# Other places in SBUF for the tiles that TensorE reads, in a one-core layer of attention, recurrence and MLP

## The chip, the cores and the metric

The kernel runs on one core of a Trainium2 chip. The metric is the device time of one execution in microseconds (us); the median of three runs is given, and lower is better.

## What is computed

One decoder layer for 256 tokens of width 1024, in fp32. All of its large products are of the form activations times weights, and the weights are 74 MB:

```python
proj = jnp.einsum("bsd,dc->bsc", u, w_in)          # 1024 x 7168
q, k, v, x_lru, g_lru, gate_attn, gate_lru = jnp.split(proj, list(SPLITS), axis=-1)
attn = moba_attention(qh, kh, to_heads(v))         # 8 heads x 128
y_attn = attn @ w_branch_attn
xc = causal_depthwise_conv(x_lru, conv_w, conv_b)
hl = rg_lru(xc, w_rg_a, b_rg_a, w_rg_i, b_rg_i, lru_lambda)
y_lru = (hl * jax.nn.gelu(g_lru)) @ w_branch_lru
merged = jax.nn.sigmoid(gate_attn) * y_attn + jax.nn.sigmoid(gate_lru) * y_lru
h = h + rms_norm(merged @ w_out, attn_post_norm[l])
u = rms_norm(h, mlp_pre_norm[l])
m = jnp.square(jax.nn.relu(u @ w_mlp_up[l])) @ w_mlp_down[l]
h = h + rms_norm(m, mlp_post_norm[l])
```

## The kernel before

**Chunks.** The weights come in 74 chunks of 1 MB, 2048 fp32 numbers on each of 128 partitions. `load` (L65) fetches a chunk into one of three `wraw` tiles. `split` (L75) cuts it exactly into an upper part `whi` (ScalarE, L89; VectorE, L87, for six chunks) and the rest `wlo` (VectorE, L90). There are three `whi` and three `wlo` tiles, used in turn, so that chunk c and chunk c + 3 have the same ones. `ahead` (L95) issues loads up to three chunks and the split one chunk before the products.

**Products.** Activations are kept as an upper and a lower part too, for instance `xgh` and `xgl` (the normed input), `xch` and `xcl` (after the convolution), `ath` and `atl` (attention), `lrh` and `lrl` (recurrence), `mgh` and `mgl` (merged), `u2` (input of the MLP, both parts side by side), `rrh` and `rrl` (the MLP's inside). A product is three matmuls of type float32r: upper with upper, and the two mixed ones. A matmul has a stationary operand of 128 columns, loaded ahead of it (PEld in the profile), and a moving operand of 256 or 512 columns, which stream through. All of them lie in SBUF as rows of fp32 along each partition.

- `three` (L152 to L155), used by `feat_chunk` (L167), the first chunk and the gates `r` and `i`: the weights are stationary and 256 tokens move: 48 matmuls with 256 columns in each chunk.
- `v_chunk` (L193) and `tok_products` (L465 to L467): activations are stationary and weights move. A chunk of `v` or of the output projection has 24 matmuls with 512 columns; one of the down projection has 18 with 512 columns and 12 with 256.
- `up_tokens` (L572 to L574): the same for the first 512 columns of the up projection. In the loop of L596 weights are stationary again; per block there is one matmul with 512 columns (L606: both parts of `u2` with `whi`) and one with 256 (L607: the upper part with `wlo`), so 16 and 16 in a chunk.

So in every chunk 12,288 columns stream through TensorE: 2048 matmuls with 256 columns and 752 with 512 in all. The scores, the transposes and the products of attention with `v` are plain fp32 and not among them.

**Places.** Five SBUF pools lie one behind the other in the order of their creation (L43 to L49): `const`, `slot` (one place for each tag `s0`, `s1`, ...; several tiles share a place at different times), `wraw`, `whi`, `wlo`; then `tmp` and `small`. Within a pool, places follow each other in the order in which they are first asked for. The sizes of the tiles alone set their addresses. A step from one block of the contraction to the next is 1024 bytes in all operands, and the second half of a chunk's output features lies 512 bytes further; so an operand's offset modulo 512 is that of its tile.

Of the kernel before, what the change touches and what calls it, by code (L numbers as in the profile page):

```python
# [9 lines left out]
F32 = mybir.dt.float32  # L10
F32R = mybir.dt.float32r
# [4 lines left out]
P = 128  # L16
T = 256
D = 1024
# [4 lines left out]
MASK_VALUE = -1e30  # L23

# chunks of weights, 1 MB each, in their order of use
# (x_lru and v in turns)
C_XL, C_V, C_Q, C_K, C_RGA, C_RGI = 0, 1, 8, 12, 16, 17
C_GL, C_GA, C_GEL, C_BA, C_BL, C_OUT, C_UPT, C_UP, C_DN = 18, 22, 26, 30, 34, 38, 42, 44, 58
NCHUNK = 74

# the part of a chunk whose upper half is taken by the vector engine instead of the scalar engine
HI_ON_VECTOR = {c: 1.0 for c in range(17, 23)}

# columns of the channel-major parameters (8 columns each)
(P_W0, P_W1, P_W2, P_W3, P_CB, P_BA, P_BI, P_LAM, P_G1, P_G2) = range(0, 80, 8)
NPAR = 80


@with_exitstack
def hybrid_layer(ctx: ExitStack, tc: tile.TileContext, head_d, x_d, w_d, cst_d, gp_d, out_d):  # L40
    nc = tc.nc

    const = ctx.enter_context(tc.tile_pool(name="const", bufs=1))  # L43
    slot = ctx.enter_context(tc.tile_pool(name="slot", bufs=1))
    wraw_p = ctx.enter_context(tc.tile_pool(name="wraw", bufs=3))
    whi_p = ctx.enter_context(tc.tile_pool(name="whi", bufs=3))
# [4 lines left out]
    ps_at = ctx.enter_context(tc.tile_pool(name="ps_at", bufs=4, space=PSUM))  # L51

    def slot_tile(i, name, dt=F32, shape=(P, KB, T)):
        return slot.tile(list(shape), dt, tag=f"s{i}", name=name)

# [5 lines left out]

# [1 line left out]
    raws, splits = {}, {}  # L63
# [7 lines left out]

    # chunks whose parts stay longer lie in tiles that are free by then
    own_slots = {C_OUT + 2: (8, 10), C_OUT + 3: (5, 6)}

    def split(c):  # L75
        raw, parts = raws.pop(c)
        if c in own_slots:
            hi, lo = (slot_tile(i, f"w{c}_{i}", F32R, (P, 2048)) for i in own_slots[c])
        else:
            hi = whi_p.tile([P, 2048], F32R, tag="whi", name=f"whi{c}")  # L80
            lo = wlo_p.tile([P, 2048], F32R, tag="wlo", name=f"wlo{c}")
        n = 2048 // parts
        for i in range(parts):
            s = slice(i * n, (i + 1) * n)
            k = i * n + int(n * HI_ON_VECTOR.get(c, 0))
            if k > i * n:
                nc.vector.tensor_copy(hi[:, i * n:k], raw[:, i * n:k])  # L87
            if k < (i + 1) * n:
                nc.scalar.copy(hi[:, k:(i + 1) * n], raw[:, k:(i + 1) * n])  # L89
            nc.vector.tensor_tensor(lo[:, s], raw[:, s], hi[:, s].bitcast(F32), ALU.subtract)  # L90
        splits[c] = (hi, lo)
# [3 lines left out]
    def ahead(c):  # L95
        """loads and splits that run ahead of the products with chunk c"""
        while state["load"] < min(NCHUNK, c + 4):
            load(state["load"])
            state["load"] += 1
        while state["split"] < min(NCHUNK, c + 2):  # L100
            with tc.high_priority():
                split(state["split"])
            state["split"] += 1

# [1 line left out]
    eps = const.tile([P, 1], F32, name="eps")  # L106
    nc.vector.memset(eps, EPS)
    first = small.tile([P, 1], F32, tag="warm", name="first")
    nc.scalar.copy(first, eps)
    # parameters, then by block of the contraction: x, features on partitions, and chunk 0 of the weights  # L110
    head = const.tile([P, NPAR + 512], F32, name="head")
# [14 lines left out]
    make_identity(nc, ident)  # L126
    # mask[q, 128 + k] = k <= q ? 0 : MASK_VALUE
    mask = const.tile([P, 2 * P], F32, name="mask")
# [8 lines left out]
    xgl = slot_tile(2, "xgl", F32R)  # L137
    whi0 = whi_p.tile([P, 2048], F32R, tag="whi", name="whi0")
    wlo0 = wlo_p.tile([P, 2048], F32R, tag="wlo", name="wlo0")
    for kb in range(KB):  # L140
        x, w = xw[kb][:, 0:T], xw[kb][:, T:512]
# [8 lines left out]

# [1 line left out]
    def three(out, wh, wl, xh, xl, start, stop):  # L152
# [4 lines left out]
    def first_chunk(xh, xl):  # L157
        """the same, block by block of the contraction, as the operands arrive"""
        hi, lo = splits.pop(0)
        banks = [mm_bank(f"mm0_{o}")[:, 0:T] for o in range(2)]  # L160
        for kb in range(KB):
            for o in range(2):
                s = slice(kb * 256 + o * P, kb * 256 + (o + 1) * P)
                three(banks[o], hi[:, s], lo[:, s], xh[:, kb, :], xl[:, kb, :], kb == 0, kb == KB - 1)
        return banks

    def feat_chunk(c, xh, xl, urgent=False):  # L167
        """two blocks of output features, [P features, 2, T]; unless what follows is urgent, the next split precedes it"""
        ahead(c + 1)
        hi, lo = splits.pop(c)  # L170
        hi = hi.rearrange("p (k c) -> p k c", k=KB)
        lo = lo.rearrange("p (k c) -> p k c", k=KB)
        bank = mm_bank(f"mm{c}").rearrange("p (o t) -> p o t", o=2)
        for o in range(2):
            for kb in range(KB):
                s = slice(o * P, (o + 1) * P)
                three(bank[:, o, :], hi[:, kb, s], lo[:, kb, s], xh[:, kb, :], xl[:, kb, :],
                      kb == 0, kb == KB - 1)
        if not urgent:
            ahead(c + 2)  # L180
        return bank

    # x_lru and the causal convolution
    PADW = T + 4
# [4 lines left out]
    xcl = slot_tile(6, "xcl", F32R)  # L189
    # v, tokens on partitions  # L190
    vt = slot.tile([P, 2, D], F32, tag="s11", name="vt")
# [61 lines left out]

    # sp8 = 8 softplus(-lam) = 8 (max(-lam, 0) + log1p(exp(-|lam|))), log1p(z) = 2 atanh(z / (2 + z))
    lam = par[:, P_LAM:P_LAM + 8]
# [23 lines left out]

    # q, k with rotary positions on features 0..31 of each head  # L280
    # (rows 0..31 of all heads are brought together as [4 x 32, 2 heads, T] for it)
    swap = list(range(16, 32)) + list(range(16))
# [19 lines left out]

    # r, i gates
    rt = slot_tile(7, "rt")
# [16 lines left out]

    # RG-LRU: a = exp(-sp8 r), mult^2 = -expm1(-2 sp8 r) = tanh(sp8 r) (1 + a^2)
    mult = slot_tile(3, "mult")
# [25 lines left out]

    # attention, one head in steps  # L350
    ath = slot_tile(12, "ath", F32R)
# [43 lines left out]

    # the three gates, with the attention of one head between chunks
    gL = slot_tile(4, "gL")
# [28 lines left out]

    # branch projections; merged = 0.5 (1 + tanh(gL / 2)) y_lru + 0.5 (1 + tanh(gA / 2)) y_attn
    mgh = slot_tile(1, "mgh", F32R)
# [18 lines left out]

# [1 line left out]
    halves = (slice(0, 512), slice(512, 1024))  # L449

    def tok_products(c0, n, act, parts):
        """act(kb) -> (hi, lo) of [P, T]; the last two chunks go one part of the result at a time"""
        acc = [[at_bank(f"acc{c0}_{b}{i}") if i < 2 else mm_bank(f"acc{c0}_{b}{i}") for i in range(len(parts[b]))]
# [31 lines left out]
    class TokenNorm:  # L485
        """1 / sqrt(mean(y^2) + eps) per token, y in parts"""

# [18 lines left out]

    # output projection, post norm, residual; then the next norm's input, features on partitions
    # (both parts of a block side by side, [P, T upper | T lower])
    u2 = [slot_tile(i, f"u2_{i}", F32R, (P, 4, 512)) for i in (12, 3)]
# [36 lines left out]
    def square_of_norm(b):  # L546
        """the norm's factor enters relu(.)^2 as its square, per token, after the down projection"""
        n = TokenNorm("h", 2)
        for i in range(2):
            r2 = n.part(i, x_tok[:, b, halves[i]])  # L550
        nc.vector.tensor_tensor(scl2[:, b:b + 1], r2, r2, ALU.mult)
# [5 lines left out]

# [1 line left out]
    rrh = [slot_tile(i, f"rrh{i}", F32R) for i in (4, 1, 2, 5)]  # L559
    rrl = [slot_tile(i, f"rrl{i}", F32R) for i in (7, 6, 8, 10)]  # L560

    # the first 512 columns with tokens on partitions, one block of tokens at a time
    ahead(C_UPT + 1)
# [69 lines left out]
def _rotary(np):  # L633
    """cosines and signed sines for rows 0..31 of a head, four times over"""
    inv = np.float32(500000.0) ** (-np.arange(0, 32, 2, dtype=np.float32) / np.float32(32))
    ang = (np.arange(T, dtype=np.float32)[:, None] * inv[None, :].astype(np.float32)).T
    cos = np.concatenate([np.cos(ang)] * 2)
    sin = np.concatenate([-np.sin(ang), np.sin(ang)])
    return np.tile(np.stack([cos, sin], axis=1), (4, 1, 1)).astype(np.float32)


def _pack(np, inp):
    """layout only: pieces of the inputs in the order and the form in which the chip reads them"""
    def a(name):
# [70 lines left out]
```

## Time and profile before

| | us |
|---|---|
| median of 3 runs | 449.8 (448.93, 449.80, 449.89) |
| span of the profiled execution | 447.7 |
| profiled execution's own time beside the median | 2.1 less: the span runs from its first to its last instruction |

The profile is of one execution. Its page gives busy time by engine, the granted clock of TensorE in 40 slices, and the chain of work that ended last. Views of the trace that are used here: the waits of one engine, and busy times in stretches of the span. The "busy" of a matmul in these views runs from its start to the modelled end of its drain, and successive matmuls overlap; how fast TensorE works is therefore read from the distance between starts, or from the length of a stretch that holds a known number of matmuls.

### The profile page before, as it was taken

The numbers are of one execution on the slowest core, as the hardware profiler recorded it, in microseconds if no ns is written. First come the engines' busy times: TensorE is split into PE (matmuls) and PEld (weight loads), VectorE is DVE, ScalarE is ACT, GpSimd is POOL, SyncE is SP. The second block draws the span as 40 slices with busy tenths as digits, with TensorE's granted clock in tenths as the row PEclk, the third lists the DMA queues.
The fourth block names the chain that finished last, engine by engine and source line by source line (L and its number), as shares of the span: only waits on it lengthen the run. The fifth ranks groups of instructions, "written<-read, shape, count | busy, mean of one in ns | idle before, by whom it ended". The sixth has DMA issues, their size and how long they took to land.

```text
span 447.7 us, 7026 instructions
## 1 busy us (share of the span) xinstructions
PE 437.3 (98%) x2916; PEld 402.2 (90%) x2916; DVE 302.2 (67%) x383; ACT 241.0 (54%) x342; POOL 21.5 (5%) x48
## 2 busy tenths in 40 slices
PE   6999999999999999999999999999999999999994
PEld 6999999999999999999998878888888888888884
DVE  5749975779997666885688566777777744444425
ACT  6686743409897575553556475555555433333322
POOL 1000073202000000000000000000000000000000
PEclk9999999999999999999999999999999999999999
DMA  8977555655634356355567703455555545455202
GB/s 269 408 286 284 180 204 206 215 202 194 208 122 167 122 194 233 120 182 189 187 219 258 277 0 132 171 190 184 192 182 188 188 182 192 184 188 193 83 1 94
DMA packets 14575, 83.59 MB, mean 187 GB/s; under 512 B 1808, under 2 KB 2576, under 8 KB 5456
## 3 DMA queue, kind: packets, MB, share of 16 engines
q1 hardware_dynamic: 13520, 80.39, 49.9%
q0 software_dynamic: 736, 2.36, 1.5%
q8 instruction: 23, 0.38, 0.3%
q10 hardware_dynamic: 288, 0.39, 0.2%
q14 instruction: 8, 0.07, 0.0%
HBM read 81.04 MB, written 1.05 MB: 183 GB/s over the span
## 4 chain that ended last, share of the span: by engine, by line
PE 97%; DMA 1%; ACT 0%; DVE 0%; issue 0%; DVEq 0%; ACTq 0%
PE mm L153 14%; PE mm L154 14%; PE mm L155 14%; PE up L606 12%; PE acc L467 8%; PE acc L466 8%; PE acc L465 8%; PE up L607 6%; PE v L204 2%; PE v L203 2%; PE v L202 2%; PE up L574 1%; PE up L572 1%; PE rg L153 1%; PE rg L155 1%; PE rg L154 1%
## 5 line engine op out<-in xcount | busy, mean ns | idle before, releaser
L90 DVE TENSOR_TENSOR wlo<-wraw,whi 128x2048 fp32r<-128x2048 f32 (+2 forms) x78 | 163.6, 2100 | 89.5 <-ACT whi L89 89.3
L89 ACT CAST whi<-wraw 128x2048 fp32r<-128x2048 f32 (+2 forms) x72 | 125.3, 1740 | 127.8 <-PE acc L467 44.4
L153 PE MATMUL mm<-xgh,whi 128*128 128x256 f32 x384 | 109.8, 290 | 4.2 <-ACT xgh L144 4.2
L154 PE MATMUL mm<-xgl,whi 128*128 128x256 f32 x384 | 109.1, 284 | 0.0
L155 PE MATMUL mm<-xgh,wlo 128*128 128x256 f32 x384 | 108.9, 284 | 0.0
L606 PE MATMUL up<-u,whi 128*128 128x512 f32 x224 | 78.9, 396 | 0.0
L153 PEld LDWEIGHTS mm<-xgh,whi 128*128 128x128 f32 x384 | 72.7, 191 | 4.6 <-ACT xgh L144 4.2
L154 PEld LDWEIGHTS mm<-xgl,whi 128*128 128x128 f32 x384 | 73.4, 191 | 0.5
L155 PEld LDWEIGHTS mm<-xgh,wlo 128*128 128x128 f32 x384 | 73.4, 191 | 0.0
L607 PE MATMUL up<-u,wlo 128*128 128x256 f32 x224 | 63.0, 281 | 0.0
L467 PE MATMUL acc<-whi,rrl 128*128 128x512 f32 (+1 forms) x160 | 56.0, 350 | 0.0
L466 PE MATMUL acc<-wlo,rrh 128*128 128x512 f32 (+1 forms) x160 | 55.8, 349 | 0.0
L465 PE MATMUL acc<-whi,rrh 128*128 128x512 f32 (+1 forms) x160 | 55.7, 348 | 0.0
L606 PEld LDWEIGHTS up<-u,whi 128*128 128x128 f32 x224 | 42.1, 188 | 9.9
L607 PEld LDWEIGHTS up<-u,wlo 128*128 128x128 f32 x224 | 42.3, 189 | 0.0
L466 PEld LDWEIGHTS acc<-wlo,rrh 128*128 128x128 f32 x160 | 30.1, 188 | 4.4
L465 PEld LDWEIGHTS acc<-whi,rrh 128*128 128x128 f32 x160 | 30.2, 189 | 4.3
L467 PEld LDWEIGHTS acc<-whi,rrl 128*128 128x128 f32 x160 | 30.1, 188 | 4.1
L153 PE MATMUL mm<-lrh,whi 128*128 128x256 f32 x64 | 18.1, 283 | 0.0
L154 PE MATMUL mm<-lrl,whi 128*128 128x256 f32 x64 | 18.1, 283 | 0.0
L155 PE MATMUL mm<-lrh,wlo 128*128 128x256 f32 x64 | 18.1, 283 | 0.0
L154 PE MATMUL mm<-atl,whi 128*128 128x256 f32 x64 | 18.0, 282 | 0.0
(197 smaller groups left out, 640.8 us busy)
## 6 DMA issues: line engine op xcount, KB each, us to landing
wraw<-in_w_dram SPq DMA_DIRECT2D x70, 1024.0 KB, 4.8
wraw<-in_w_dram SPq DMA_DIRECT2D x8, 256.0 KB, 6.5
xw_a<-in_head_dram SPq DMA_DIRECT2D x4, 256.0 KB, 3.9
wraw<-in_w_dram SPq DMA_DIRECT2D x2, 512.0 KB, 7.0
x_tok<-in_x_dram SPq DMA_DIRECT2D x1, 1024.0 KB, 9.2
gp<-in_gp_dram POOLq DMA_DIRECT2D x1, 1024.0 KB, 4.6
xw_b<-in_head_dram SPq DMA_DIRECT2D x3, 256.0 KB, 4.6
out_dram<-res ACTq DMA_DIRECT2D x2, 192.0 KB, 2.0
```

The costliest lines, as they stand in the source:

```text
L89: nc.scalar.copy(hi[:, k:(i + 1) * n], raw[:, k:(i + 1) * n])
L90: nc.vector.tensor_tensor(lo[:, s], raw[:, s], hi[:, s].bitcast(F32), ALU.subtract)
L153: nc.tensor.matmul(out, wh, xh, start=start, stop=False)
L154: nc.tensor.matmul(out, wh, xl, start=False, stop=False)
L155: nc.tensor.matmul(out, wl, xh, start=False, stop=stop)
L202: nc.tensor.matmul(banks[b], xgh[:, kb, s], hi[:, k, :], start=kb == 0, stop=False)
L203: nc.tensor.matmul(banks[b], xgh[:, kb, s], lo[:, k, :], start=False, stop=False)
L465: nc.tensor.matmul(out, xh[:, s], hi[:, hs], start=first, stop=False)
L466: nc.tensor.matmul(out, xh[:, s], lo[:, hs], start=False, stop=False)
L467: nc.tensor.matmul(out, xl[:, s], hi[:, hs], start=False, stop=last)
L606: nc.tensor.matmul(bank, hi[:, kb, c], u2[kb // 4][:, kb % 4, :], start=kb == 0, stop=False)
L607: nc.tensor.matmul(bank[:, 0:T], lo[:, kb, c], u2h(kb, slice(0, T)), start=False, stop=kb == KB - 1)
```

## The change

The change allots unused gaps in front of some tiles, and makes the `whi` and `wlo` tiles 64 bytes (16 numbers) longer than what is used of them, so that the three places of each step by 64 bytes modulo 1024. No instruction, shape, wait or order on any engine is different; only SBUF addresses are. Gaps are counted in units of 32 bytes.

```diff
+GAPS = {"const": 1, "s10": 4, "s8": 8, "s12": 1, "whi": 15, "wlo": 26}
+W_STEP = 16
...
+    def gap(pool, tag):
+        if tag in GAPS:
+            pool.tile([P, 8 * GAPS[tag]], F32, tag="gap_" + tag, name="gap_" + tag, bufs=1)
+    laid = set()
     def slot_tile(i, name, dt=F32, shape=(P, KB, T)):
+        if i not in laid:
+            laid.add(i)
+            gap(slot, f"s{i}")
         return slot.tile(list(shape), dt, tag=f"s{i}", name=name)
...
+    gap(const, "const")
+    gap(whi_p, "whi")
+    gap(wlo_p, "wlo")
...
+    def weight_tiles(c):
+        hi = whi_p.tile([P, 2048 + W_STEP], F32R, tag="whi", name=f"whi{c}")
+        lo = wlo_p.tile([P, 2048 + W_STEP], F32R, tag="wlo", name=f"wlo{c}")
+        return hi[:, 0:2048], lo[:, 0:2048]
...
-            hi = whi_p.tile([P, 2048], F32R, tag="whi", name=f"whi{c}")
-            lo = wlo_p.tile([P, 2048], F32R, tag="wlo", name=f"wlo{c}")
+            hi, lo = weight_tiles(c)
...
-    whi0 = whi_p.tile([P, 2048], F32R, tag="whi", name="whi0")
-    wlo0 = wlo_p.tile([P, 2048], F32R, tag="wlo", name="wlo0")
+    whi0, wlo0 = weight_tiles(0)
```

Where the tiles begin, in bytes of a partition modulo 1024, worked out from the sizes of all tiles in front of them:

| tiles | before | after |
|---|---|---|
| `whi`, `wlo`, chunks 0, 3, 6, ... | 224 | 128 |
| `whi`, `wlo`, chunks 2, 5, 8, ... | 224 | 192 |
| `whi`, `wlo`, chunks 1, 4, 7, ... | 224 | 256 |
| `xgh`, `xgl`, `mgh`, `mgl`, `atl`, second half of `u2`, three of the four `rrh` | 96 | 128 |
| `xch`, `xcl`, `lrh`, `lrl`, the last `rrh`, one `rrl` | 224 | 256 |
| two `rrl` | 224 | 384 |
| one `rrl` | 224 | 640 |
| `ath`, first half of `u2` | 224 | 672 |

The three sequences of chunks hold up to chunk 39; two later chunks of the output projection lie in places of `slot`, and from chunk 42 on the numbers are shifted. Before, all of these offsets leave 32 modulo 64; after, all but 672 are multiples of 64.

## Rows read from the trace of the kernel before

**Rows 1.** The page: span, busy time of each engine (share, instructions), TensorE's granted clock, chain.

```profile
span 447.7 us, 7026 instructions
...
PE 437.3 (98%) x2916; PEld 402.2 (90%) x2916; DVE 302.2 (67%) x383; ACT 241.0 (54%) x342; POOL 21.5 (5%) x48
...
PEclk9999999999999999999999999999999999999999
...
PE 97%; DMA 1%; ACT 0%; DVE 0%; issue 0%; DVEq 0%; ACTq 0%
```

**Rows 2.** All waits of TensorE: waiter, released by, us in total, times, longest.

```profile
PE mm L153 <- ACT xgh L144: 4.2, 1, 4.2
```

**Rows 3.** Stretches: us from:to, length, busy by engine (instructions), clock, DMA, GB/s.

```profile
core 0: us, PE busy (x) PEld busy (x) DVE busy (x) ACT busy (x) POOL busy (x), PEclk, DMA share, GB/s
4.23:12.43 8.20, 8.20 (x49) 8.06 (x50) 7.14 (x18) 6.91 (x17) 0.72 (x1) 1.00 0.99 330
12.43:18.00 5.57, 5.57 (x27) 4.52 (x26) 4.29 (x7) 3.89 (x7) 0.00 (x0) 1.00 1.04 407
52.25:97.81 45.56, 45.56 (x385) 45.56 (x384) 31.45 (x33) 18.16 (x16) 15.42 (x33) 1.00 0.59 203
196.50:213.46 16.96, 16.96 (x146) 16.96 (x145) 10.84 (x9) 6.70 (x5) 0.00 (x0) 1.00 0.51 184
219.21:236.49 17.28, 17.28 (x147) 17.28 (x146) 14.24 (x12) 9.06 (x7) 0.00 (x0) 1.00 0.63 236
236.49:242.06 5.57, 5.57 (x27) 4.52 (x26) 5.32 (x5) 4.45 (x4) 0.00 (x0) 1.00 0.57 204
295.61:346.25 50.64, 50.64 (x291) 44.20 (x290) 37.42 (x46) 27.62 (x36) 0.00 (x0) 1.00 0.53 188
357.49:419.31 61.82, 61.82 (x332) 52.82 (x331) 26.22 (x13) 21.53 (x12) 0.00 (x0) 1.00 0.51 186
419.31:430.39 11.08, 11.08 (x62) 9.63 (x61) 4.58 (x2) 3.82 (x2) 0.00 (x0) 1.00 0.00 0
441.61:447.70 6.09, 0.00 (x0) 0.00 (x0) 2.10 (x5) 0.86 (x3) 0.00 (x0) 0.88 0.25 86
```

**Rows 4.** The page's costliest groups, the split: line, engine, tiles, count, busy, mean ns, idle before.

```profile
L90 DVE TENSOR_TENSOR wlo<-wraw,whi 128x2048 fp32r<-128x2048 f32 (+2 forms) x78 | 163.6, 2100 | 89.5 <-ACT whi L89 89.3
L89 ACT CAST whi<-wraw 128x2048 fp32r<-128x2048 f32 (+2 forms) x72 | 125.3, 1740 | 127.8 <-PE acc L467 44.4
```

## The prediction

> **What bounds the kernel now.** I read the page first [rows 1]: TensorE is busy 437.3 us of a span of 447.7, its clock is granted in full in every slice, and 97% of the chain that ended last is TensorE. Then its waits [rows 2]: one, of 4.2 us, for the first operand. So no other engine, transfer or semaphore is late after the start, and the change touches none of them. What is left is how fast TensorE works while it never waits for a semaphore, and the busy columns don't tell that, because successive matmuls overlap. The length of stretches with a known number of matmuls does [rows 3]. Every chunk streams 12,288 columns; at one column per clock of 2.4 GHz that is 5.12 us. The stretches give, for each chunk:
>
> - 48 matmuls with 256 columns, `xgh` and `xgl` at 96, weights at 224: 45.56 / 8 = 5.695 us, or 118.6 ns for each matmul, 12.0 over the 106.7 ns of its columns;
> - the same with `ath` at 224 and `atl` at 96: 16.96 / 3 = 5.653 us, 117.8 ns, 11.1 over;
> - the same with `lrh` and `lrl` at 224, as the weights: 17.28 / 3 = 5.76 us, 120.0 ns, 13.3 over;
> - 24 matmuls with 512 columns, activations at 96 and weights at 224: 5.57 us in `v` and in the output projection, 232.1 ns, 18.8 over 213.3;
> - up projection (16 and 16): 50.64 / 9 = 5.627 us; down projection (18 with 512, 12 with 256): 61.82 / 11 = 5.62; its last chunks, where all tiles lie at 224: 11.08 / 2 = 5.54.
>
> Two things are in this table. First, matmuls of one shape cost 117.8, 118.6 or 120.0 ns, with the same instructions and no wait; the places of their tiles differ. VectorE's share rises in the same order (64, 69 and 82% of these stretches), so these three rows alone don't separate the two; the down projection does, with 42 and 41% of VectorE and 5.62 and 5.54 us. So places do matter a little. Second, where all offsets are equal, the excess belongs to a matmul and not to its columns: with 120.0 ns for each of the 12 short ones, the 18 long ones of the last chunks take (5.54 - 1.44) / 18 = 227.8 ns, 107.8 for the further 256 columns, one clock each. The excess of 13.3 ns is 32 clocks.
>
> Summed over the kernel, the excess is 24 chunks x 0.575 (`x_lru`, q, k, gates) + 4 x 0.533 (attention's branch) + 6 x 0.64 (`r`, `i`, the recurrence's branch) + 10 x 0.45 (`v`, output, first part of up) + 14 x 0.507 + 12 x 0.50 + 4 x 0.42 = 39.1 us. That is all that places can give back. The columns themselves (74 x 5.12 = 378.9 us), the start, attention and the last 6.09 us without TensorE [rows 3] stay.
>
> **The change part by part.** Instructions, waits and order are the same, so each step is a change of the 39.1 us.
>
> *Weights and features at several distances from each other.* Before, they are 0 or 128 apart (modulo 512). After, weights at 128, 192 and 256 stand against features mostly at 128: 0, 64 and 128 apart, each for a third of the chunks. The rows price 0 (120.0 and 227.8 ns) and 128 (118.6 and 232.1); 64 is not in the trace, and I take the middle. The mean is 119.3 and 230.0 ns. For each chunk that is 48 x 119.3 = 5.726 against 5.695 (+0.031, 24 times), 5.653 (+0.073, 4 times) and 5.76 (-0.034, 6 times); 24 x 230.0 = 5.52 against 5.57 (-0.05, 10 times); 5.589 against 5.627 (-0.038, 14 times); 5.572 against 5.62 (-0.048, 12 times) and 5.54 (+0.032, 4 times). The sum is -0.6 us: by distances alone, almost nothing. For this step I count 0.
>
> *All but `ath` and half of `u2` now begin at a multiple of 64 bytes.* Before, every tile that these products read leaves 32 modulo 64. This the trace cannot show, since no operand of theirs lies otherwise; the bounds are nothing and all of the excess. What speaks for it is the form of the excess: a fixed number of clocks for each matmul whatever its length, as from something that happens at the ends of an operand. A row of 256 numbers is 1024 bytes, 16 pieces of 64 bytes; begun in the middle of a piece it touches 17, and a row of 512 touches 33 and not 32. If TensorE takes a row in such pieces and one passes in 16 clocks (16 numbers, one a clock), the piece too many costs 16 clocks = 6.7 ns in each matmul. A slice of stationary columns (512 bytes) touches 9 pieces for 8, and if that cost as much again, both would make up the 32 clocks of the stretches with equal offsets. That other stretches have only 11.1 ns makes me count one piece and not two. It is a guess at a mechanism, sized by rows. The moving operand begins at a multiple of 64 in all of the 2800 matmuls except 128 with `ath` and 224 with the first half of `u2`: 2448 x 6.7 ns = 16.3 us. From this I take off 0.3 us for the first chunk, whose 8.20 us [rows 3] are set by the arrival of its blocks. Sum: -16.0 us. A chunk with 48 short matmuls gains 0.32 us, one with 24 long ones 0.16.
>
> *Cover for a faster TensorE.* A chunk must still be split while the one before it is multiplied: VectorE's part takes 2.1 us, ScalarE's 1.7 [rows 4]. The fullest stretch is the first chunk of the output projection, VectorE busy 5.32 of 5.57 us [rows 3]; at 5.57 - 0.16 = 5.41 it still fits. Next is the recurrence's branch with 14.24 of 17.28 us, 4.75 for a chunk of then 5.44. Loads: 1 MB in 5.37 us is 195 GB/s, and 407 were reached [rows 3]. So nothing else becomes late; if VectorE did at the fullest place, it would cost a few tenths of a us. ScalarE and VectorE write and read the same tiles at the new places; nothing in the trace ties their times to a place, and with 54% and 67% busy [rows 1] a few per cent either way are hidden.
>
> The span becomes 447.7 - 16.0 = 431.7 us, and with the 2.1 us by which the median is above the span: **433.8 us**.
>
> The Trainium skill speaks against any effect. "TensorE: Matmul & The Clock Gate", Part 2, on LDWEIGHTS, says that TensorE has two independent read ports in SBUF and that loading the next weights takes no bandwidth from the running matmul; by that rule places don't count and the time stays at 449.8 us, which is the second rival below. The 117.8, 118.6 and 120.0 ns of one shape [rows 3] do not agree with it. The same page ("Wait — 56ns, not 53.3ns?") gives a fixed 2.5 ns for each matmul above its columns; by it, as an estimate, 7 of the 39.1 us could never be given back.
>
> **The rivals.**
>
> *More than one piece is given back.* If the stationary slices' extra piece counts too, 2448 x 13.3 = 32.6 us go: 417 us. For it: 32 clocks are two pieces exactly. Against: 11.1 and 12.0 ns are less than two pieces, so two can't be paid in each of those matmuls.
>
> *Only distances count, or nothing does.* Then the sum of the first step holds, 449.2 us, or 449.8. For it: distances are all that rows show to matter, and by little. That the change doesn't do what it says belongs here: the gaps are never written, but they take their room, and the addresses move as the table shows; so only an effect can be missing.
>
> *The new distance is worse.* Every third chunk has its weights at 192, 64 bytes from the features at 128, a distance that no row prices. If the two reads get in each other's way there as they do for long matmuls at 128, an excess of 18.8 instead of 12.0 ns, a third of the matmuls lose 6.8 ns: 933 x 6.8 = 6.3 us, 456.1 us. It decides once three successive chunks of q and k take over 17.1 us (3 x 5.695) together. For it: long matmuls at a distance of 128 are worse than at 0 while short ones are better, so the sign of such an effect can't be told beforehand. Against: no stretch is near it for short matmuls.
>
> **How the numbers follow.** One piece given back, in whole or for the most part (427 to 441 us): 0.48. More than that (below 427): 0.13. Distances alone (449.2, about 447 to 451): 0.14, half of it within 0.2%. Nothing (449.8): 0.10. Worse (451 to 460): 0.15. Likeliest is 433.8, with 427 to 441 as its own range. A measurement of this kernel tells 0.2%, 0.9 us, from no change. Faster by more: 0.48 + 0.13 + 0.05 = 0.66; the same: 0.07 + 0.10 = 0.17; slower: 0.15 + 0.02 = 0.17. For 8 in 10 the range goes from 421, which leaves out half of the second case (0.06), to 452, which leaves out most of the last (0.11). It is wide because the main term has no row of its own.
>
> **What the profile after would show.** Right: the stretch of q and k at about 43.0 us for its eight chunks and not 45.56, with little difference between thirds; `v` and the first output chunk at 5.41; attention's branch gaining only in its products with `atl` (a third of 0.32 us for a chunk); in the up loop the half with `u2` at 672 as slow as before and the other faster; TensorE's clock in full, and no new wait of TensorE. One chunk in three fast and two not would say that distances act and not multiples of 64. `ath` gaining as much as the rest would refute the piece of 64 bytes; so would a gain of long matmuls that is twice that of short ones. Chunks with weights at 192 longer than the rest would be the last rival.

## The result: 446.6 us

| | median, us | runs |
|---|---|---|
| before | 449.39 | 448.93 to 449.89 |
| after | 446.61 | 446.41 to 446.83 |
| ratio | 0.9931 | 95% interval 0.9916 to 0.9945 |

Predicted were 433.8 us, with 421 to 452 as the range. The direction was right; the gain was 2.8 us and not 16.

The page of the changed kernel answers to [rows 1]; its four kinds of line are span, busy time by engine, TensorE's granted clock in 40 slices, and the chain that ended last.

```profile
span 444.7 us, 7026 instructions
...
PE 434.4 (98%) x2916; PEld 400.0 (90%) x2916; DVE 301.9 (68%) x383; ACT 240.5 (54%) x342; POOL 20.9 (5%) x48
...
PEclk9999999999999999999999999999999999999998
...
PE 97%; DMA 1%; ACT 0%; DVE 0%; issue 0%; DVEq 0%; ACTq 0%
```

All waits of TensorE in it, as in [rows 2]:

```profile
PE mm L175 <- ACT xgh L166: 4.2, 1, 4.2
```

The same count of instructions, the same clock row but for one slice, the same single wait, and 2.9 us less of busy TensorE: the kernel is bound as before and TensorE works a little faster. The stretches, with the columns of [rows 3]:

```profile
51.51:96.74 45.23, 45.23 (x386) 45.23 (x384) 31.32 (x33) 18.13 (x16) 14.82 (x33) 1.00 0.60 205
194.70:211.67 16.97, 16.97 (x146) 16.97 (x145) 10.83 (x9) 6.68 (x5) 0.00 (x0) 1.00 0.50 187
217.43:234.53 17.10, 17.10 (x146) 17.10 (x145) 14.24 (x12) 8.93 (x7) 0.00 (x0) 1.00 0.61 231
234.53:240.05 5.52, 5.52 (x27) 4.52 (x26) 5.19 (x5) 4.53 (x4) 0.00 (x0) 1.00 0.60 227
293.32:343.66 50.34, 50.34 (x290) 44.10 (x289) 37.43 (x47) 27.60 (x36) 0.00 (x0) 1.00 0.53 188
354.88:416.15 61.27, 61.27 (x333) 52.81 (x332) 26.21 (x13) 21.48 (x12) 0.00 (x0) 1.00 0.52 188
```

In order: q and k, 45.23 us for eight chunks (before 45.56 [rows 3]); `ath`, 16.97 (16.96); `lrh`, 17.10 (17.28); the first output chunk, 5.52 (5.57); nine chunks of the up loop, 50.34 (50.64); eleven of the down projection, 61.27 (61.82). No stretch gains more than 1.1%. Another 0.6 us of the profiled execution is the first chunk, 7.61 us against 8.20. It isn't set by the arrival of its blocks, as the prediction had it: TensorE waits for nothing in it after its start. Its matmuls with 256 columns start 0.21 us apart at first, which is one column per clock of 1.2 GHz, and 0.12 us apart later; by then TensorE had worked without a wait since 4.2 us. In the changed kernel (start, length, operation):

```profile
7.77 0.37 PE L177 MATMUL mm<-xgh,wlo 128*128 128x256 f32 x1
7.98 0.28 PE L176 MATMUL mm<-xgl,whi 128*128 128x256 f32 x1
8.10 0.28 PE L177 MATMUL mm<-xgh,wlo 128*128 128x256 f32 x1
```

Before, the same step comes at 9.3 us, after 22 matmuls and not 16; the PEclk row doesn't show it. In the other executions below the clock rose at 7.2 to 10.0 us, and the first chunk took between 7.4 and 8.4. So this 0.6 us is when the higher clock came, and not places; the places made the other 2.4 us of the span's 3.0.

Four successive chunks of q and k, one by one (us from:to, length, busy TensorE, clock, share of DMA, GB/s), show where the gain of q and k is:

```profile
51.51:57.17 5.66, 5.66 (x50) 1.00 0.53 190
57.17:62.92 5.75, 5.75 (x50) 1.00 0.61 198
62.92:68.61 5.69, 5.69 (x50) 1.00 0.54 193
68.61:74.07 5.46, 5.46 (x50) 1.00 0.58 218
```

Chunk 8, weights at 192, takes 5.66; chunk 9, at 128, 5.75; chunk 10, at 256, 5.69; chunk 11, at 192 again, 5.46. So the fast chunk belongs to one third of the chunks, but not all of that third is fast: the two with weights at 192 differ from each other, 117.8 against 113.7 ns a matmul, with the same code at the same addresses modulo 1024.

### The profile page after: what moved, and what is told of

Its sections match the earlier page's. It is cut to its first block, busy times and chain, and to the rows that moved or that the text cites. A ratio compares the mean times of both kernels' runs of the same rounds, so it can differ in the third digit from the quotient of the medians.

```text
span 444.7 us, 7026 instructions
## 1 busy us (share of the span) xinstructions
PE 434.4 (98%) x2916; PEld 400.0 (90%) x2916; DVE 301.9 (68%) x383; ACT 240.5 (54%) x342; POOL 20.9 (5%) x48
## 4 chain that ended last, share of the span: by engine, by line
PE 97%; DMA 1%; ACT 0%; DVE 0%; issue 0%; DVEq 0%; ACTq 0%
PE mm L175 14%; PE mm L176 14%; PE mm L177 14%; PE up L628 12%; PE acc L489 8%; PE acc L487 8%; PE acc L488 8%; PE up L629 6%; PE v L224 2%; PE v L225 2%; PE v L226 2%; PE up L596 1%; PE up L594 1%; PE rg L177 1%; PE up L595 1%; PE rg L176 1%
## 5 line engine op out<-in xcount | busy, mean ns | idle before, releaser
L177 PE MATMUL mm<-ath,wlo 128*128 128x256 f32 x64 | 18.0, 281 | 0.0
```

Of the source, the lines that this page charges most:

```text
L177: nc.tensor.matmul(out, wl, xh, start=False, stop=stop)
```

## The experiments

A *distance* here is the offset of the weights less that of the features, modulo 256 bytes; a *rate* is the mean time from the start of one matmul with 256 columns to the next in a chunk. Diffs are against the changed kernel, unless the text says otherwise, and leave out lines where `...` stands and the old values of `GAPS` and `W_STEP` after the first. A time without a range is of one execution; there the rates in its trace are what is read. In the kernels from e5_fine0 on (but not e7_next, e9_half, e13_split0 and e14_split1) a chunk's weights may also start inside a longer tile:

```diff
-W_STEP = 16
+W_STEP = 64
+W_OFF = {0: (16, 16), 1: (0, 0), ...}   (chunk: first element of hi, of lo)
...
-        return hi[:, 0:2048], lo[:, 0:2048]
+        h, l = W_OFF[c]
+        return hi[:, h:h + 2048], lo[:, l:l + 2048]
```

**Multiples of 64 bytes alone (e1_align).** All tiles move up by 32 bytes, so that everything begins at a multiple of 64 and every distance is that of the kernel before.

```diff
-GAPS = {"const": 1, "s10": 4, "s8": 8, "s12": 1, "whi": 15, "wlo": 26}
-W_STEP = 16
+GAPS = {"const": 1}
+W_STEP = 0
```

> All tiles move by 32 bytes together: every offset becomes a multiple of 64, every distance between a weight tile and a feature tile stays as in the kernel before. Theory of the prediction (a 64-byte piece too many in each matmul): 2800 x 6.7 ns = 18.7 us go, about 431 us, the eight chunks of q and k in 43.0 us and not 45.56. Rival (only distances modulo 512 count): same as before within 0.2%, 449.4 us, and the eight chunks in 45.5 to 45.6 us.

Measured: 449.14 us, ratio to before 0.9991 (0.998 to 1.0001). Q and k, and `lrh`, in its trace (us from:to, length, busy TensorE, clock, share of DMA, GB/s, as in all the stretches that follow unless more engines are named):

```profile
52.31:97.88 45.57, 45.57 (x386) 1.00 0.60 203
219.28:236.56 17.28, 17.28 (x147) 1.00 0.65 240
```

Each is within 0.01 us of its row in [rows 3], as are `ath`, the up loop and the down projection. A beginning at a multiple of 64 bytes is worth nothing.

**One distance for all (e2_d64).** All features at 128 modulo 512, all weights at 192 (but for two chunks of the output projection in places of `slot`).

```diff
+GAPS = {"const": 1, "s5": 12, "whi": 2}
+W_STEP = 0
```

> All features at 128 modulo 512, all whi and wlo at 192: 64 apart throughout. Distances: the changed kernel's chunks with 256 columns at that distance took 113.4 to 113.7 ns for a matmul, some 117.8; the eight chunks of q and k take 43.6 us if all are of the fast kind, 45.2 if none is, and the kernel 438 to 445 us. Multiples of 64: nothing is different from the changed kernel but ath and u2, 446.6 us less 1 to 2, and chunks of q and k not below its mean.

Measured: 439.49 us, ratio 0.9777 (0.976 to 0.9794), 7 us faster than the changed kernel. The six stretches that are shown above of the changed kernel, in the same order and columns:

```profile
51.36:94.90 43.54, 43.54 (x385) 43.54 (x384) 31.44 (x33) 18.16 (x16) 15.24 (x33) 1.00 0.62 212
190.00:206.32 16.32, 16.32 (x146) 16.32 (x145) 11.09 (x10) 6.76 (x5) 0.00 (x0) 1.00 0.56 196
211.76:228.08 16.32, 16.32 (x146) 16.32 (x145) 13.57 (x12) 8.60 (x6) 0.00 (x0) 1.00 0.60 218
228.08:233.58 5.50, 5.50 (x27) 4.51 (x25) 4.89 (x7) 4.76 (x4) 0.00 (x0) 1.00 0.74 298
287.03:337.91 50.88, 50.88 (x291) 44.19 (x290) 37.42 (x46) 27.60 (x36) 0.00 (x0) 1.00 0.52 186
349.04:409.32 60.28, 60.28 (x332) 52.15 (x331) 26.36 (x13) 21.45 (x12) 0.00 (x0) 1.00 0.54 192
```

Q and k need 5.44 us a chunk and `ath` and `lrh`, 117.8 and 120.0 ns before, come to the same 113.3 ns. The excess over 106.7 ns is 6.7 ns, 16 clocks, half of the 32 at distance 0. Long matmuls don't follow: 5.50 us for the 24 of the output chunk are 229 ns, 15.8 over 213.3, and at distance 0 they have 14.5 in the last chunks of [rows 3]. The down projection gains 2.5%, the up loop loses 0.5%. VectorE is busy 68% of `ath` and 83% of `lrh` here (11.09 and 13.57 of 16.32 us), as different as before (64 and 82% [rows 3]), and the rates are now equal; so VectorE's share isn't what set 117.8 and 120.0.

**Thirds at 32, 64, 96 and at 160, 192, 224 (e3_sw32, e4_sw160).**

```diff
+GAPS = {"const": 1, "s5": 12, "whi": 1, "wlo": 13}   # e4_sw160: "whi": 5
+W_STEP = 8
```

> Features at 128, the three weight tiles at distances 32, 64 and 96, so that chunks 0, 3, ... / 2, 5, ... / 1, 4, ... price one distance each. Distances: three different chunk times, 64 again at 113.4 to 113.7 or 117.8 ns, 32 and 96 on either side of it, somewhere between 107 and 120 ns. Multiples of 64: distance makes no difference, but stationary slices at 32 and 96 begin in the middle of a piece; if that costs, those two thirds are slower than the 64 one by up to 6.7 ns a matmul.

> The same with distances 160, 192 and 224. Distances: each third has its own time; none of the three is in a trace so far, anything from 107 to 120 ns for a matmul with 256 columns. Multiples of 64: 160 and 224 equal, 192 the faster.

Measured: 446.16 and 448.24 us. Chunks 8 to 10 of e3_sw32 (distances 64, 32, 96), and then of e4_sw160 (192, 160, 224):

```profile
51.77:57.23 5.46, 5.46 (x50) 1.00 0.62 197
57.23:62.91 5.68, 5.68 (x51) 1.00 0.63 195
62.91:68.67 5.76, 5.76 (x50) 1.00 0.61 205
```

```profile
52.14:57.80 5.66, 5.66 (x50) 1.00 0.52 190
57.80:63.56 5.76, 5.76 (x51) 1.00 0.65 205
63.56:69.16 5.60, 5.60 (x51) 1.00 0.53 187
```

Of six distances only 64 is fast. 64 and 192 (64 the other way) are not alike: 5.46 and 5.66 us.

**Steps of 16 bytes (e5_fine0, e6_fine256).** A distance of its own for nearly every chunk, all features at 128 in the first and at 128 and 256 in the second.

```diff
+W_OFF = {..., 8: (0, 0), 9: (0, 0), 10: (4, 4), 11: (8, 8), 12: (8, 8), 13: (12, 12), ...}
```

> Features at 128 modulo 512; each chunk's weights are put at another distance, in steps of 16 bytes from 0 to 256 (one in three chunks: 256 to 512), by a start inside a longer tile. Distances: each chunk of q, k and gates has its own time, those at 0, 32, 64, 96, 160, 192, 224 again near 120.0, 118.4, 113.4, 120.0, 119.9, 117.9, 116.7 ns for a matmul; between 48 and 80 a valley around 113.4 if the effect is wide, 113.4 at 64 alone if it goes with multiples of 64. Prediction's theory (multiples of 64 alone): all chunks at a multiple of 64 alike, which the runs before have already shown to be wrong for 0 and 64.

> The same from 256 to 512, with one chunk in three from 0 to 256, for the chunks of q, k and the gates (features at 128); other features lie at 256. Distances: if nearness alone counts, 448 (that is 64 below) mirrors 64 and takes 113.4 or 117.8 ns, as two chunks of the changed kernel did; 256 to 384 in no trace so far, 107 to 120 ns.

Measured: 448.26 and 448.69 us. In nine of ten pairs of e5_fine0, distances of d and d + 256 gave the same rate within 0.2 ns, as in chunks 14 (320) and 15 (64):

```profile
86.32:91.77 5.45, 5.45 (x51) 1.00 0.61 203
91.77:97.21 5.44, 5.44 (x51) 1.00 0.56 205
```

Both at 113.3 to 113.4 ns; the period is 256 bytes. The tenth pair, chunk 20 at 384 (120.0) and 21 at 128 (118.6), has two rates that distance 128 shows in the kernel before as well. In e5_fine0 the rate at 0 and 256 was 120.0 to 120.2, at all others between 116.7 and 123.4.

**Whose distance (e7_next).** Weights 64 from the features that they are multiplied with in one matmul of three, at 0 in the second and at 128 in the third, but placed so that each moving operand lies 64 from the slice of weights that is loaded beside it.

```diff
+GAPS = {"const": 1, "s2": 2, "whi": 12, "wlo": 2}
+W_STEP = 0
```

> xgh at 128, xgl and whi at 192, wlo at 256. If what counts is the distance of the moving operand to the stationary slice that is loaded beside it, for the matmul after it, all three matmuls of a product have 64 and the eight chunks of q and k take 43.5 us. If it is the distance to the matmul's own stationary operand, the three have 64, 0 and 128, and the chunks take 45 to 45.8 us.

Measured: 448.99 us, 45.49 us for q and k, 118.3 to 118.7 ns in every chunk with `xgh` and `xgl` behind the first. The distance to the next slice alone doesn't make the fast rate. It is no plain mean over the three matmuls either: (113.3 + 120.0 + 118.6) / 3 = 117.3.

**Unequal pairs (e8_pairs).** `whi` and `wlo` of a chunk at different distances, and steps of 4 bytes around 64.

```diff
+W_OFF = {..., 8: (16, 16), 9: (14, 14), 10: (15, 15), ..., 17: (16, 48), ..., 32: (13, 13), 33: (19, 19), ...}
```

> Features at 128; upper and lower weights of a chunk now at different distances (modulo 256), and, for chunks with both alike, steps of 4 bytes around 64. Theory: the excess comes from the stationary slice read beside a moving row, with a period of 256 bytes. Then 64 with 64 takes 113.4 ns again, and a chunk with only one of the two at 64 lies between 113.4 and 120 ns. Rival: 64 is good only when all operands keep one distance (the reads stay in step); then every mixed chunk takes 117 to 120. The width of the valley: 48 and 80 took 117.8 to 123.4 and 118.7, so 56 and 72 are expected half way, about 116, unless the valley is as narrow as a few bytes.

Measured: 447.85 us. Chunks 8 (64 and 64), 32 (52) and 33 (76):

```profile
53.70:59.35 5.65, 5.65 (x49) 1.00 0.59 200
202.44:207.91 5.47, 5.47 (x51) 1.00 0.55 196
207.91:213.35 5.44, 5.44 (x50) 1.00 0.55 194
```

Here the distance 64 was slow (117.8 ns) and 52 and 76 were fast (113.4 to 113.5), while 56, 60, 68 and 72 gave 117.6 to 119.3. Chunks 17 and 18, with one part at 64 and the other at 192, ran at 113.3 to 113.4, as fast as 64 with 64 elsewhere. No order by distance fits that. As a price list the run decides nothing; it shows that a chunk's rate isn't a function of its own distance.

**Half a load (e9_half).** In the kernel before, the third matmul of `three`, except the last of an accumulation, uses 64 of the 128 stationary columns; this leaves out half of that part of the product.

```diff
-        nc.tensor.matmul(out, wl, xh, start=False, stop=stop)
+        if stop:
+            nc.tensor.matmul(out, wl, xh, start=False, stop=True)
+        else:
+            nc.tensor.matmul(out[0:64], wl[:, 0:64], xh, start=False, stop=False)
```

> The kernel before with half of the stationary columns (64 of 128) in the third matmul of each product with weights stationary, but for the last of an accumulation; the other half of that small correction is left out. If the excess is the price of reading the stationary slice beside the moving row, the recurrence's branch (all offsets equal, 120.0 ns, 32 clocks each) loses 16 clocks in one of three matmuls: 17.28 us for three chunks become 17.0. If it is a fixed cost of a matmul or of its moving row, 17.28 stays.

Measured: 447.59 us. Q and k, `lrh` and the up loop, which has no such matmul:

```profile
52.19:97.39 45.20, 45.20 (x386) 1.00 0.59 204
217.64:234.56 16.92, 16.92 (x147) 1.00 0.64 229
293.72:344.36 50.64, 50.64 (x291) 1.00 0.52 187
```

`lrh` goes from 17.28 to 16.92 us with as many moving columns: 0.36 us by 3 x 14 shortened matmuls, 8.6 ns each. Q and k lose 0.36 us too, by 8 x 14 of them, 3.2 ns each. The up loop stays. So part of the excess hangs on how many stationary columns are loaded, or on how many rows come out; this run changes both, and which of them it is stays open. That the shorter matmul only shifts the others against each other, as the later runs do, isn't excluded either.

**The best distance for each loop (e10_best).** 64 for chunks with 256 columns and for the down projection, 0 for `v`, output and the token blocks, 96 for the up loop.

```diff
+W_OFF = {..., 7: (0, 0), 8: (16, 16), ..., 44: (24, 24), ..., 58: (16, 16), ...}
```

> The distances that were best in the runs before, by kind of chunk: 64 where weights are stationary with 256 columns, 0 in v, the output projection and the first part of up, 96 in the up loop, 64 in the down projection. By their chunk times: against all at 64 (439.5 us) the up loop gains 14 x 32 x 3.4 ns = 1.5 us, v and output 0.3 us: 437.7 us, 2.7% under the kernel before. If chunk times depend on what went before (two kinds were seen at one distance), 437 to 441.

Measured: 440.62 us (439.74 to 440.86), ratio 0.979 (0.9774 to 0.9805): no better than e2_d64, and 2.9 us over the 437.7 that was expected, but inside the 437 to 441 given for rates that hang on what went before. Q and k, and nine chunks of the up loop:

```profile
52.21:97.43 45.22, 45.22 (x385) 1.00 0.60 205
289.35:339.27 49.92, 49.92 (x290) 1.00 0.52 190
```

The up loop does what was expected (49.92 against 50.88 us). But the chunks 8 to 18, at the distance 64 of e2_d64, all run at 117.8 ns: 1.68 us lost in q and k alone. From chunk 19 on they run at 113.3; between chunks 18 and 19 stand the first matmuls of attention (0.47 us from start to start, without a wait of TensorE).

**What came before, or a hitch (e11_mode, e12_split).** Against e10_best: `v`, output and token chunks at 64 too; or the second matmul of chunk 8 in four pieces of 64 columns, and nothing else.

```diff
+                if c == 8 and o == 0 and kb == 0:
...
+                    for q in range(4):
+                        t = slice(64 * q, 64 * q + 64)
+                        nc.tensor.matmul(bank[:, o, t], hi[:, kb, s], xl[:, kb, t], start=False, stop=False)
```

> The kernel of e10_best with one thing changed: the weights of the v, output and token chunks (512 columns) lie 64 bytes from the features as well, and not at 0. In e10_best the chunks 8 to 18 ran at 117.8 ns a matmul, in e2_d64 at 113.3, with the same distance 64 in both; before them stood a v chunk at distance 0 in e10_best and at 64 in e2_d64. Theory A (a distance of 64 allows two rates, and what ran just before chunk 8 decides which one holds until the next stop): chunks 8 to 18 at 113.3 again, so e10_best less 11 chunks x 48 x 4.5 ns = 2.4 us and 0.4 us in chunks 2 and 6, plus 0.2 us in the 512-column chunks: about 438.0 us. Rival B (something else of e10_best, such as the start inside a longer tile, made 117.8): 117.8 stays, about 440.8 us. Both: up loop 173.3 ns, down loop 182.7 ns.

> The kernel of e10_best with one thing changed: the second matmul of chunk 8 (256 columns) is written as four of 64 columns, with the same addresses and the same result. It costs about 0.1 us by itself, since a weight load of 128 columns no longer hides behind 64. Theory A (the two rates at distance 64 are two phases of one steady pattern, and a hitch can change the phase, as chunks 19, 27 and 30 of e10_best follow a stop and run at 113.3): chunks 8 to 18 at 113.3 or at another rate than 117.8; with 113.3, 440.6 - 2.4 + 0.1 = about 438.3 us. Rival B (the rate hangs on distances and on whole chunks before, not on the phase): 117.8 stays in chunks 8 to 18, about 440.7 us.

Measured: 439.17 us (438.28 to 442.21), ratio 0.9774 (0.9748 to 0.9801), and 438.77 us (437.52 to 439.78), ratio 0.9755 (0.9734 to 0.9775). TensorE's starts in time (start, length, operation) at the beginning of chunk 8, first in e10_best:

```profile
52.21 0.28 PE L177 MATMUL mm<-xgh,whi 128*128 128x256 f32 x1
52.33 0.28 PE L178 MATMUL mm<-xgl,whi 128*128 128x256 f32 x1
52.44 0.28 PE L179 MATMUL mm<-xgh,wlo 128*128 128x256 f32 x1
```

and in e12_split from the four pieces on:

```profile
52.47 0.53 PE L205 MATMUL mm<-xgl,whi 128*128 128x64 f32 x4
52.83 0.37 PE L206 MATMUL mm<-xgh,wlo 128*128 128x256 f32 x1
53.03 0.28 PE L177 MATMUL mm<-xgh,whi 128*128 128x256 f32 x1
53.16 0.28 PE L178 MATMUL mm<-xgl,whi 128*128 128x256 f32 x1
53.27 0.28 PE L179 MATMUL mm<-xgh,wlo 128*128 128x256 f32 x1
53.38 0.28 PE L177 MATMUL mm<-xgh,whi 128*128 128x256 f32 x1
```

Steps of 0.12 us in the first; in the second, once the pieces are through, of 0.11. Chunk 8, and then the chunks 9 to 15 together with what remains, in e12_split:

```profile
52.35:58.15 5.80, 5.80 (x53) 1.00 0.61 196
58.15:96.22 38.07, 38.07 (x338) 1.00 0.62 213
```

38.07 / 7 = 5.44 us a chunk, 113.3 ns, and it stays so to chunk 18. One hitch (the matmul in pieces), which made its own chunk 0.15 us longer than in e10_best, took 0.21 us off each of the ten behind it (5.44 against 45.22 / 8 = 5.65), at the same addresses. In e11_mode the chunks 8 to 18 run at 113.3 as well; but there the chunks 21 to 28, each behind matmuls of attention, fell to 117.8, which ate 1.6 us of the gain, and the time came out 1.2 us over the expectation of 438.0. So at a distance of 64 there are two rates, an interruption of the stream by other matmuls or pieces can select one, and it holds until the next.

What decides which rate comes is not known, and e11_mode doesn't show that it is the distance in the chunk before. All operands of e2_d64 and of e11_mode have the same offsets modulo 256 in every chunk up to 43. Yet chunk 2, behind a `v` chunk at 64 in both, ran at 113.4 ns in the first and at 117.8 in the second, and chunks 22 to 24, with attention between them, took 7.10 us each in e2_d64 (first line) and 7.29 in e11_mode:

```profile
131.54:152.83 21.29, 21.29 (x179) 1.00 0.36 128
131.38:153.26 21.88, 21.88 (x179) 1.00 0.40 143
```

Each kernel has one trace, so whether its next execution has the same rates in the same chunks isn't shown either.

**Is it the phase alone? (e13_split0, e14_split1, e15_fine).** *Phase* stands here for what an interruption changes at unchanged addresses. The same four pieces in chunks 8 and 34 of the kernel before; in chunks 8, 23, 26 and 35 of the changed kernel; in every chunk of e5_fine0 with features on partitions.

```diff
+                if c in (8, 34) and o == 0 and kb == 0:        # e13_split0
+                if c in (8, 23, 26, 35) and o == 0 and kb == 0:  # e14_split1
+                if o == 0 and kb == 0:                         # e15_fine
```

> The kernel before, no tile moved, with the second matmul of chunk 8 and of chunk 34 written as four of 64 columns. In e12_split this one hitch took eleven chunks from 117.8 to 113.3 ns a matmul; the first split chunk was about 0.3 us longer for it. Theory A (the distance between the two tiles decides which rates exist, and the phase decides which of these holds; at the distances of the kernel before, 113.3 isn't among them): chunks 8 to 15 stay at 118 to 120 ns and chunks 34 to 37 at 120.0, the time at 449.7 + 0.5 = about 450.2 us. Rival B (the phase alone decides, and the moved tiles only happened to change it): chunks 9 to 15 and 35 to 37 fall to 113.3, 10 chunks x 48 x 5.5 ns = 2.6 us off, about 447.6 us.

> The changed kernel with the second matmul of the chunks 8, 23, 26 and 35 written as four of 64 columns. These four have their weights 64 bytes from the features, as chunks 11 and 14 do, and ran at 117.8 ns a matmul there where 11 and 14 ran at 113.7. Theory A (phase at one distance): they fall to about 113.5, 4 x 48 x 4.3 = 0.8 us off, against about 4 x 0.3 us for the splits: about 447.0 us. The sum says little, the rate in the four chunks decides. Rival B (these four are slow by their place, the work beside them or the chunk ahead of them): 117.8 stays, about 447.8 us.

> The kernel of e5_fine0 (a distance of its own for each chunk, in steps of 16 bytes) with the second matmul of every chunk with features on partitions written as four of 64 columns, so that each chunk begins with a hitch and no phase is inherited. Theory A (the price list of e5_fine0 is one of distances, and only 64 modulo 256 has a fast phase): the list stays within about 1 ns, 113.4 at 64 and 320, 116.7 to 123 elsewhere. Rival B (the list was one of inherited phases): other distances show 113 to 114 as well. The time itself is only that of the 27 or so splits, some 7 us more than e5_fine0 (448.26) unless the rates fall.

Measured: 450.26 us, ratio 1.0011 (1.0 to 1.0023); 448.17 us, ratio 0.9959 (0.9947 to 0.9972); 458.44 us. In e13_split0, chunks 9 to 15, and `lrh` with its first matmuls in pieces one chunk ahead:

```profile
57.87:97.75 39.88, 39.88 (x339) 1.00 0.59 203
219.48:236.76 17.28, 17.28 (x147) 1.00 0.62 229
```

5.70 us a chunk and 17.28 us, as in [rows 3]: without moved tiles the hitch gives nothing. In e14_split1 the chunks 8, 23 and 26 fell from 117.8 to 113.4, and 35 stayed at 117.7. That one has its features at 256, so its distance is 192 and not 64; the expectation had overlooked the sign. The time missed its expectation by 1.2 us. With the pieces chunk 8 took 5.80 us against 5.66, so the faster rate didn't pay for them; and in the profiled execution chunk 2 had the slow rate and chunk 4 took 6.53 us against 6.00, of it 0.5 us of waiting for a split. In e15_fine the chunks at 64 and 320 ran at 113.3 again, those at 0 and 256 at 119.8 to 120.0, and the rest between 116.6 and 120.1. So no other distance of this list got the fast rate from a hitch. But the list didn't stay within 1 ns as expected: 123.4 at 48 became 117.7, 120.0 at 240 became 117.2, and three chunks at 96 and 224 moved by 1.1 to 2.8 ns, so 64 isn't the only distance with more than one rate. The time, 10.2 us over e5_fine0 and not some 7, puts 0.33 us on each of the 31 split chunks.

The rates of the chunks from 6 to 37 whose weights and features have one distance, in the sixteen kernels without e9_half (the first four matmuls of a chunk and hitches left out; the most frequent distances):

| distance | chunks | rate, ns |
|---|---|---|
| 0 | 52 | 120 in all |
| 32 | 19 | 118.2 to 118.4 |
| 64 | 156 | 113 to 114 in 129, 118 in 27 |
| 96 | 15 | 117.3, 118.7 or 120.0 |
| 128 | 87 | 119 in 78, 120 in 8, 118 in 1 |
| 160 | 18 | 119.7 to 120.1 |
| 192 | 20 | 117.7 to 117.8 in 18, 113.4 in 2 |
| 224 | 16 | 116.7 to 116.8 in 15, 117.8 in 1 |

So the rates that a chunk showed go with its distance, and what came before can choose among them.

## Why the prediction was wrong in size

*TensorE without waits sets the end, and what places can give back is in its excess over the columns*: right. The page and the one wait of after say so; e1_align leaves the excess and the time as they were, and in e2_d64 the time falls with the excess.

*Multiples of 64 bytes, 2448 x 6.7 ns = 16.3 us*: this is the step that failed. e1_align makes just this change and gives nothing. The prediction said that the trace had no row for it and put 0.48 on it because the excess looked like something fixed at the ends of an operand. That form holds where it was read, at distance 0 (13.3 ns for short matmuls, 14.5 for long ones), and not at 64, where they have 6.7 and 15.8 (e2_d64). And a fixed cost at the ends says nothing on which property of the address sets it: the runs show the distance, 6.7 ns at 64 against 13.3 at 0 for short matmuls. "`ath` gaining as much as the rest would refute the piece" was the wrong test as well: nothing gained, and `ath` with it (16.97 us).

*Distances alone, -0.6 us*: the right step, counted at 0. Its working holds within 0.03 us a chunk in five of seven lines. It gave 5.52 us for the output chunk (measured 5.52), 5.589 for the up loop (50.34 / 9 = 5.593), 5.572 for the down projection (61.27 / 11 = 5.570; its last chunks 5.57, 11.14 / 2), 5.726 for `lrh` (5.70), but 5.726 for q and k (5.654) and for `ath` (5.657). Part of that is luck. The step's 5.52 is a mean of three thirds and the output chunk shown is one of the third at 64, and half of the up loop's matmuls read the half of `u2` at 160 modulo 256, at distances of 32, 96 and 224, which the step hadn't priced, as it hadn't for the matmuls with `ath`. What was mis-sized is one term, short matmuls at 64, taken as the middle, 119.3 ns: they measured 113.3 to 113.7 or 117.8. With the measured rates this step alone accounts for the result, but for the first chunk: by the starts of the chunks in the two traces, the span's -3.0 us are q and k -0.33, `r`, `i` and the first gate chunk -0.25, the other gates and attention -0.48, `ath` +0.01, `lrh` -0.17, the output projection and the tokens before the up loop -0.23, the up loop's 14 chunks -0.42, the down projection's first 14 -0.49, the chunks 1 to 7 -0.11, the first chunk -0.59, and +0.06 at the two ends.

*The first chunk*: the 0.3 us taken off for it rested on a wrong reading. Its 8.20 us are not set by arrival, and the clock was not full from the start: the starts 0.21 us apart show 1.2 GHz until 9.3 us.

*Cover for a faster TensorE*: right here, TensorE has no new wait. Two readings in it were off without effect: the 2.1 and 1.7 us are means over three forms, and a whole chunk's split takes VectorE 2.29 us and ScalarE 1.91. In six of the traces, though, not in that of the changed kernel, TensorE waits once for the split of chunk 4 (e12_split 1.5 us, e8_pairs 1.4, e10_best and e7_next 1.2, e14_split1 0.5, e2_d64 0.3). A faster TensorE isn't shown as the cause, since e7_next with a span of 447.2 us has the wait and e11_mode with 437.4 has none. In e7_next the chain leads through ScalarE back to the transfer of `x_tok`, which took 10.7 us there and 9.1 in e11_mode.

*The rival of a worse new distance*: the sign was wrong for short matmuls. 64 is the fastest distance of the table; the worst rate in any chunk was 123.4 ns, once at 48. *Distances only*: this happened, and it had 0.14; the time fell just below the 447 to 451 that it gave. *More than one piece*: not seen; 113.3 ns is the lowest rate that any chunk showed.

*The list of signs*: "one chunk in three fast and two not would say that distances act" is what chunks 9 to 11 above show. The list told the cases apart even where the chances didn't.

The Trainium skill's rule in "TensorE: Matmul & The Clock Gate", Part 2, that the loading of weights takes nothing from the running matmul, does not agree with e9_half (120.0 ns become 117.5 with half a load in a third of the matmuls, with the reserve given there) nor with e2_d64: by that rule moved tiles would leave the time at 449.8 us, and 439.5 were measured. Which part of TensorE takes the time isn't shown.

## What to carry to other kernels

Where TensorE has no wait left, compare the time from start to start of equal matmuls across the kernel: different rates of one shape are a lead, and a move of the tiles by some tens of bytes tests it without another change. Price an unknown address by moving one thing alone before a mechanism is built on it. A price list made chunk by chunk isn't safe where a chunk may inherit the rate of the one before it; run one setting through the whole kernel, and look at all of its chunks.

## What was unexpected

- Moving tiles alone, with no instruction changed, took 2.2% off this kernel (e2_d64, 439.49 us); with other distances in the up loop and one matmul in four pieces it was 438.77 us. The intervals of e2_d64, e11_mode and e12_split overlap; all three beat both kernels.
- The rate repeats with 256 bytes, not with the 1024 that the change counts in, and its sign matters: 113.3 at 64, mostly 117.8 at 192.
- A shape can have two steady rates at one address, 113.3 and 117.8 ns. A single split matmul took the stream from the slow one to the fast one, and a rate held over eleven chunks, 62 us in e10_best.
- The best distance hangs on the shape: 64 for chunks of short matmuls and for the down projection, but in the up loop 173.3 ns a matmul at 96 (49.92 us for nine chunks) against 176.7 at 64 (50.88), and for long matmuls alone 227 ns at 0 against 229 at 64.
- What inside TensorE makes the 16 and 32 clocks was not found. e7_next and e8_pairs exclude that a single distance alone decides, whether to the operand of the same matmul or to the slice that is loaded next.
